# A hybrid decoder layer on one core: another order of the front, two-byte lookups, projection weights in column halves

## The chip, the core and the metric

The kernel runs on one core of one Trainium2 chip. A core has five engines with queues of their own: TensorE (PE in the profile, its weight loads PEld), VectorE (DVE), ScalarE (ACT), GpSimd (POOL) and SyncE (SP), which here only issues DMAs. The engines meet through semaphores; each works off its own instructions in the order in which the program put them. The metric is the device time of one execution in microseconds, as the median of repeated runs; beside it one execution was profiled.

## The reference, cut to what matters

One layer of a decoder over 512 tokens of width 1024, with 16 learned meta tokens in front. It has two residual sub-layers. The mixing sub-layer is an RMS norm, one input projection whose columns feed two groups, and one output projection:

```python
u = rmsnorm(h, norm_mix_w)
z, xbc, dt_raw, conf_in = split(u @ w_in)
y_ssd = ssd_mixer(z, xbc, dt_raw, ...)       # 16 heads in 4 groups, chunks of 128 tokens
y_conf = conformer_conv(conf_in, ...)        # a * sigmoid(g), causal conv of width 31,
                                             # LayerNorm over 1024 channels, swish
h = h + concat([y_ssd, y_conf]) @ w_out
h = h + peer_ffn(rmsnorm(h, norm_ffn_w), ...)
```

The SSD group convolves x, B and C with a width of 4, scans over chunks, multiplies by silu(z) and normalizes within each of its 4 groups. The channel sub-layer is a product-key lookup: for each token and each of 8 heads, the 16 best of 128 keys on either of two sides, then the 16 best of the 256 sums of these, give 16 of 16384 experts:

```python
v1, i1 = top_k(s1, 16); v2, i2 = top_k(s2, 16)
cand = v1[..., :, None] + v2[..., None, :]
top_s, pos = top_k(cand, 16)                 # expert = 128 * i1[row] + i2[column]
gate = softmax(top_s)
y = sum over experts of gelu(x . w_down[e]) * gate * w_up[e]
```

A final RMS norm ends the layer.

## The kernel before

Every large product is done in three matmuls of a reduced fp32 form: both operands are split in a high part and a remainder, and mm3 (lines 159 to 162) multiplies high by high, high by rest and rest by high into one PSUM bank. Weights are split by wsplit (line 176): SP loads the raw block, ACT copies it to the high part (line 181) and writes its negative to the low part (182), and a DMA that POOL issues adds the raw block again from DRAM to the low part (183). There are two raw and two split buffers, taken in turn.

The order of work inside each engine is not written by hand. The program calls its operations in an order, gives some of them a higher or lower priority (early and late), and a planner with a cost model arranges each engine's queue; DMAs stand in the queue of the engine that issues them. The stages are:

1. Start (lines 187 to 282). Five token tiles (four of 128 and the meta tokens, in the order MO) are loaded, normalized and transposed to uT. The z weights of group 0 and the dt columns are loaded apart and split by z_split (203).
2. Projection blocks in the order of the list ORDER (44): z0 to z3 (z_block, 312: tokens as rows, 256 columns of one group, then silu), x0 to x7 (x_block, 349: channels as rows; 0 to 3 are x, 4 and 5 are B, 6 and 7 are C, with the convolution of width 4 on DVE, lines 361 and 362) and c0 to c7 (c_block, 397: 128 gate and 128 value channels, then GLU at 406 and 407, then 30 taps on DVE, line 413, and sums for the LayerNorm, all marked late). The matmuls of x and c blocks come from proj_ct (285). An SSD group (ssd, 501) is called as soon as its x and z blocks and x4 to x7 are there; its operations are marked early. A group's result goes to DRAM, yD (548).
3. Output (590 to 670). y_split (587 on) transposes and splits y; out_part(b) (608) multiplies a quarter of the mixed channels by a quarter of w_out and adds it into h1 at 620. Parts 0 and 1 take SSD groups 0 and 1, then 2 and 3, read back from yD. Parts 2 and 3 take the conformer channels after the LayerNorm (638 to 663). Then comes the second norm with transposes (581) and splits (264).
4. Queries (775 to 792): product with the keys and the first top 16 by top16 (742: two passes of MAX8 at 743 and 746, FIND_INDEX8 at 744 and 747, MATCH_REPLACE8 at 745).
5. second(t) (825), for each token tile: the sums of a staircase of 50 candidates per head (pairs, 813) in two tables, scores and expert numbers; the top 16 of the scores; then the expert numbers of the 16 places by a one-hot compare with 0 to 49 (836), a product with the table of numbers (838) and a sum (839), in two halves of 3200 elements.
6. Gate maps (916): for tokens of tiles 0 to 2 a dense 128 x 128 map of gates per token is built from two-byte one-hots (924 to 927) by small matmuls (932, 933). Tile 3 goes another way: single experts are gathered by POOL (873) and applied on DVE (889, 896), some between gate maps.
7. All experts (986 on) for tiles 0 to 2: down projection (753) and up projection (963). 88 of the 128 down blocks are done ahead, with high priority, from stage 5 on.

The layout matters in one place: the split output operands (hl, 574) share memory with uT, so that no output part can be prepared before the last projection has read uT.

Of the kernel before, what the change touches and what calls it, by code (L numbers as in the profile page):

```python
# [43 lines left out]
ORDER = "z0 x4 x5 x6 x7 x0 c0 c1 x1 c2 x2 c3 z1 x3 c4 c5 z2 c6 z3 c7".split()  # L44
# [21 lines left out]
def pack(inputs):  # L66
# [9 lines left out]
    for k in range(8):  # L76
        blocks.append(np.concatenate([w_in[:, ca + 128 * k:ca + 128 * k + 128],
                                      w_in[:, cg + 128 * k:cg + 128 * k + 128]], 1))
    wb = np.stack(blocks)
    win = ac(wb.reshape(19, 8, 128, 256).transpose(0, 2, 1, 3))  # L80
# [37 lines left out]
def body(ctx, tc, I, out):  # L118
# [57 lines left out]
    def wsplit(raw, src, n=2048):  # L176
# [4 lines left out]
        S.activation(wh, raw, AF.Copy)  # L181
        S.activation(wl, wh.bitcast(F32), AF.Copy, scale=-1.0)
        G.dma_start(wl, src, accum_op=OP.add)
        return wh, wl
# [5 lines left out]
    load(xt[0], I["x"][0:128])  # L190
    cst = con(C_N)
    load(cst, I["cst"])
    load(wmix, bcast(I["nw"][0], 1024))
    zraw = mem(F0, 2176)
    zsrc = I["wzdt"].rearrange("p c n -> p (c n)")
    load(zraw[:, :1088], zsrc[:, :1088])
    load(xm[:NM], I["meta"])
    load(zraw[:, 1088:], zsrc[:, 1088:])
# [17 lines left out]
    def next_w():  # L216
        while worder and len(raws) < 2:
            src = I["win"][worder.pop(0)].rearrange("p c n -> p (c n)")
            raws.append((wload(src), src))
        raw, src = raws.pop(0)  # L220
        return wsplit(raw, src)
# [43 lines left out]

    for n, t in enumerate(MO):
# [7 lines left out]
        for half in range(2):  # L274
# [7 lines left out]
            split_to(uTh[:, half * 4:half * 4 + 4, c0:c0 + parts], uTl[:, half * 4:half * 4 + 4, c0:c0 + parts], pv)  # L282


    def proj_ct(wh, wl, j):
        p0, p1 = ps("pa"), ps("pa")
        for dc in range(8):
            sh = wh[:, dc * 256 + j * 128:dc * 256 + j * 128 + 128]
            sl = wl[:, dc * 256 + j * 128:dc * 256 + j * 128 + 128]
# [5 lines left out]
    A0 = S0 + 5120  # L295
    XS = [mem(o, 1280).rearrange("p (c n) -> p c n", c=5) for o in (A0, S0)]
    ZB = [mem(o, 1024).rearrange("p (t n) -> p t n", t=4) for o in (A0 + 1280, S0 + 1280)]
# [9 lines left out]
    yD = dram.tile([4, 128, 1024], F32, name="yD")  # L307


    dtraw = con(80)  # L310

    def z_block(k):
        if k == 0:
            zn = 272
            wh, wl = zsplit
        else:
            zn = 256
            wh, wl = next_w()
        for t in MO if k == 0 else range(4):
            p = ps("pa")  # L320
            c0 = NM + 128 * t if t >= 0 else 0
            z0 = 0 if t >= 0 else 256
            for dc in range(8):
                mm3(p[:, z0:zn], uTh[:, dc, c0:c0 + 128], uTl[:, dc, c0:c0 + 128],
                    wh[:, dc * zn + z0:dc * zn + zn], wl[:, dc * zn + z0:dc * zn + zn], dc == 0, dc == 7)
            if k == 0:
                V.tensor_copy(dtraw[:, 16 * (t + 1):16 * (t + 2)], p[:, 256:272])
            if t < 0:
                continue
            zt = ZB[k % 2][:, t, :]  # L330
            S.activation(zt, p[:, :256], AF.Tanh, scale=0.5)
            V.scalar_tensor_tensor(zt, zt, 1.0, p[:, :256], op0=OP.add, op1=OP.mult)
# [64 lines left out]
    def c_block(k):  # L397
        wh, wl = next_w()
        g0, g1 = proj_ct(wh, wl, 1)
        S.activation(sig[:, 0:272], g0[:, :272], AF.Tanh, scale=0.5)  # L400
        S.activation(sig[:, 272:528], g1[:, :256], AF.Tanh, scale=0.5)
        a0, a1 = proj_ct(wh, wl, 0)
# [99 lines left out]
    def ssd(g):  # L502
# [4 lines left out]
        for c in range(5):  # L507
# [11 lines left out]
            if c > 0:  # L519
# [18 lines left out]
                y_ = ybs[n % 3]  # L538
# [9 lines left out]
                load(yD[c - 1, :, 256 * g:256 * g + 256], y_)  # L548
# [36 lines left out]
    yh = [mem(B0 + 512 * k, 512) for k in range(4)]  # L585
# [22 lines left out]
    def out_part(b):  # L608
        for hf in range(2):
            po = [ps("pa") for _ in range(4)]  # L610
            src = I["wout"][hf, b].rearrange("p k n -> p (k n)")
            wh, wl = wsplit(wload(src), src)
            for t in range(4):
                for k in range(4):
                    sh, sl = hl((b % 2) * 4 + k)
                    mm3(po[t], sh[:, 128 * t:128 * t + 128], sl[:, 128 * t:128 * t + 128],
                        wh[:, 512 * k:512 * k + 512], wl[:, 512 * k:512 * k + 512], k == 0, k == 3)
            for t in range(4):
                hh = h1[t][:, 512 * hf:512 * hf + 512]
                V.tensor_tensor(hh, hh, po[t], op=OP.add)  # L620

    with early(YP):
        n = 0
        for g in range(2):
            for t in range(4):
                load(yq[n % 4], yD[t, :, 256 * g:256 * g + 256])
                y_split(yq[n % 4], t, g, 1)
                n += 1
        for t in range(4):
            load(h1[t], I["x"][128 * t:128 * t + 128])  # L630
        out_part(0)
        for t in range(4):
            load(yh[t], yD[t, :, 512:1024])
            y_split(yh[t], t, 2, 2)
        out_part(1)


    with early(LNP):
        p = ps()
        for c0, (a_, b_) in ((0, (sumd, convo[:, 7, :])), (4, (sumq, sq7[0]))):  # L640
            for t in range(4):
                ts = slice(128 * t, 128 * t + 128)
                E.matmul(p[:, c0 + t:c0 + t + 1], a_[:, ts], ones[:, 0:1], start=True, stop=False)
                E.matmul(p[:, c0 + t:c0 + t + 1], b_[:, ts], ones[:, 0:1], start=False, stop=True)
        mom = stat(8)
        V.tensor_scalar(mom, p[:, 0:8], 1.0 / D, None, op0=OP.mult)
        dl = mom[:, 0:4]
# [19 lines left out]
    out_part(2)  # L667
    out_part(3)
# [41 lines left out]
    idxf = v5(rmem(1024))  # L710
    cS = rmem(400).rearrange("p (h k) -> p h k", h=8)
    cI = rmem(400).rearrange("p (h k) -> p h k", h=8)
    h16 = lambda a: a.rearrange("p (h k) -> p h k", h=8)
    ts_, posu, posf, gate, ef, ei, i1f, i2f = [rmem(128) for _ in range(8)]
# [5 lines left out]
    oneh = mem(P0, 3200).rearrange("p (h k c) -> p h k c", h=4, k=16)  # L720
# [92 lines left out]
    def pairs(eng, o, A, B, op=OP.add):  # L813
        off = 0
        for a in range(5):
            nb = 16 // (a + 1)
            eng.tensor_tensor(o[:, :, off:off + nb], A[:, :, a:a + 1].to_broadcast([128, 8, nb]), B[:, :, 0:nb], op=op)
            off += nb
        eng.tensor_tensor(o[:, :, off:off + 6].rearrange("p h (a b) -> p h a b", a=3),
                          A[:, :, 5:8, None].to_broadcast([128, 8, 3, 2]),  # L820
                          B[:, :, None, 0:2].to_broadcast([128, 8, 3, 2]), op=op)
        off += 6
        eng.tensor_tensor(o[:, :, off:off + 8], A[:, :, 8:16], B[:, :, 0:1].to_broadcast([128, 8, 8]), op=op)

    def second(t):
        V.tensor_copy(idxf[:, t], idxu[:, t])
        V.tensor_scalar(idxf[:, t, 0], idxf[:, t, 0], 128.0, None, op0=OP.mult)
        pairs(V, cS, vals[:, t, 0], vals[:, t, 1])
        pairs(V, cI, idxf[:, t, 0], idxf[:, t, 1])
        for h in range(8):  # L830
            top16(cS[:, h, :], ts_[:, 16 * h:16 * h + 16], posu.bitcast(U32)[:, 16 * h:16 * h + 16],
                  mrb[h % 4][:, 0:50])
        V.tensor_copy(posf, posu.bitcast(U32))
        for hf in range(2):
            hs = slice(4 * hf, 4 * hf + 4)
# [204 lines left out]
```

## Time and profile before

| what | value |
|---|---|
| median of 3 runs | 1749.32 us (1747.53 to 1750.86) |
| the profiled execution | 1744.54 us, its span 1742.8 us |
| granted TensorE clock, mean | 0.969 |
| PE busy | 1642.9 us, 94% of the span |
| DVE busy | 1446.8 us, 83% |
| ACT busy | 767.2 us, 44% |
| POOL busy | 394.3 us, 23% |

A row of a group gives line, engine, operation, output and input, shapes and count, then the busy time and the mean of one in nanoseconds, then idle time before it. A row of the timeline gives start and duration in microseconds, then the instruction, and in brackets the idle time before it and what ended it. Instructions of one engine overlap a little at their ends, so that durations are slightly longer than the distance of two starts. A busy PE is not a PE at its peak: the count of its matmuls in a stretch says how fast it went.

### The profile page before, as it was taken

How to read it: one execution, taken by the hardware profiler on the slowest of the kernel's cores; microseconds unless marked ns; L12 is line 12 of the kernel's file. 1: busy time of each engine (PE TensorE's matmuls, PEld its weight loads, DVE VectorE, ACT ScalarE, POOL GpSimd, SP SyncE). 2: the span in 40 equal slices, each digit the busy share in tenths (PEclk: the TensorE clock that was granted, in tenths of full speed). 3: DMA queues.
4: the chain of work that ended last, by engine and by line, in shares of the span. 5: the costliest groups of instructions: out<-in, count | busy, mean ns of one | idle time of the engine just before them, and what ended most of it. 6: DMA issues, size and time to landing. Idle time of an engine off the chain costs nothing.

```text
span 1742.8 us, 26076 instructions
## 1 busy us (share of the span) xinstructions
PE 1642.9 (94%) x9529; PEld 1485.8 (85%) x9529; DVE 1446.8 (83%) x2873; ACT 767.2 (44%) x1117; POOL 394.3 (23%) x317
## 2 busy tenths in 40 slices
PE   6999999758989999989999999999999999999997
PEld 6999899637778899979988988888888899999996
DVE  4559999995359999999888988888888888888885
ACT  5655555434333334424655873333333333333333
POOL 1001011110000002423333003223222255444540
PEclk9999999867999999989999999999999999999999
DMA  6766567443532346768897789999999999999992
GB/s 207 170 156 155 130 153 186 135 117 82 145 106 73 97 159 232 265 211 284 296 310 288 271 290 375 342 347 364 343 341 366 325 322 364 345 351 342 327 333 81
DMA packets 163025, 426.43 MB, mean 245 GB/s; under 512 B 14144, under 2 KB 80960, under 8 KB 154832
## 3 DMA queue, kind: packets, MB, share of 16 engines
q1 hardware_dynamic: 122144, 262.22, 42.9%
q0 software_dynamic: 40752, 162.55, 30.2%
q8 instruction: 74, 1.21, 0.3%
q14 instruction: 55, 0.45, 0.1%
HBM read 382.24 MB, written 42.47 MB: 244 GB/s over the span
## 4 chain that ended last, share of the span: by engine, by line
PE 74%; DMA 10%; DVE 6%; issue 5%; ACT 3%; POOL 2%; SPq 0%; POOLq 0%; DVEq 0%; ACTq 0%
PE pa L162 16%; PE pa L161 16%; PE pa L160 16%; PE pb L162 6%; PE pb L160 6%; PE pb L161 6%; DMA MR<-win 3%; DVE M L413 3%; DMA M<-wu,M 3%; POOL M L873 1%; DMA MR<-wout 1%; PE pb L932 1%; PE pb L933 1%; DMA M<-wd,M 1%; PE pb L786 1%
## 5 line engine op out<-in xcount | busy, mean ns | idle before, releaser
L161 PE MATMUL pa<-MR 128*128 128x512 f32 (+3 forms) x2120 | 729.0, 344 | 5.1 <-DMA MR<-wout 5.1
L160 PE MATMUL pa<-MR 128*128 128x512 f32 (+3 forms) x2120 | 728.8, 345 | 5.3 <-ACT M L761 2.5
L162 PE MATMUL pa<-MR 128*128 128x512 f32 (+3 forms) x2120 | 690.2, 345 | 10.0 <-DVE MR L739 6.1
L162 PEld LDWEIGHTS pa<-MR 128*128 128x128 f32 x2120 | 402.4, 190 | 43.1 <-DVE MR L739 6.6
L160 PEld LDWEIGHTS pa<-MR 128*128 128x128 f32 x2120 | 404.1, 191 | 37.4 <-ACT M L761 3.4
L161 PEld LDWEIGHTS pa<-MR 128*128 128x128 f32 x2120 | 403.5, 190 | 36.3 <-DMA MR<-wout 6.3
L738 ACT ACTIVATE MR<-M 128x1024 fp32r<-128x1024 f32 (+1 forms) x264 | 286.0, 1084 | 289.9 <-PE pa L161 122.0
L739 DVE TENSOR_TENSOR MR<-M,MR 128x1024 fp32r<-128x1024 f32 (+1 forms) x264 | 329.3, 1250 | 45.2 <-ACT MR L738 44.3
L873 POOL DMA_INDIRECT M<-wd,M x128 | 171.4, 1339 | 491.5 <-DVE M L889 229.3
L873 POOL DMA_INDIRECT M<-wu,M x128 | 173.6, 1356 | 363.7 <-DVE M L896 215.5
L160 PE MATMUL pb<-MR 128*128 128x384 f32 (+1 forms) x576 | 206.9, 359 | 0.0
L161 PE MATMUL pb<-MR 128*128 128x384 f32 (+1 forms) x576 | 206.6, 359 | 0.0
L162 PE MATMUL pb<-MR 128*128 128x384 f32 (+1 forms) x576 | 205.5, 359 | 0.0
L959 ACT ACTIVATE MR<-M 128x384 fp32r<-128x384 f32 x128 | 66.9, 523 | 264.8 <-issue 208.4
L896 DVE SCALAR_TENSOR_TENSOR M<-M 128x1024 f32<-128x1024 f32 x128 | 163.6, 1278 | 17.9 <-DMA M<-wu,M 17.6
L413 DVE SCALAR_TENSOR_TENSOR M<-M 128x512 f32<-128x512 f32 x240 | 170.6, 740 | 2.4 <-ACT M L411 2.2
L889 DVE SCALAR_TENSOR_TENSOR M<-M 128x1024 f32<-128x1024 f32 x128 | 154.4, 1216 | 6.4 <-DMA M<-wd,M 6.3
L960 DVE TENSOR_TENSOR MR<-M,MR 128x384 fp32r<-128x384 f32 x128 | 71.0, 556 | 59.1 <-ACT MR L959 59.1
L161 PEld LDWEIGHTS pb<-MR 128*128 128x128 f32 x576 | 108.1, 188 | 11.4
L160 PEld LDWEIGHTS pb<-MR 128*128 128x128 f32 x576 | 108.1, 188 | 11.3
L935 ACT ACTIVATE M<-pb 128x512 f32<-128x512 f32 x96 | 97.0, 1159 | 46.2 <-PE pb L933 43.5
L162 PEld LDWEIGHTS pb<-MR 128*128 128x128 f32 x576 | 108.1, 188 | 10.4
(217 smaller groups left out, 1521.4 us busy)
## 6 DMA issues: line engine op xcount, KB each, us to landing
M<-wdT SPq DMA_DIRECT2D x128, 512.0 KB, 5.1
M<-wu SPq DMA_DIRECT2D x128, 512.0 KB, 6.7
GD<-M SPq DMA_DIRECT2D x40, 512.0 KB, 6.2
M<-GD SPq DMA_DIRECT2D x32, 640.0 KB, 7.9
M<-win SPq DMA_DIRECT2D x19, 1024.0 KB, 4.8
MR<-win POOLq DMA_DIRECT2D x19, 1024.0 KB, 8.2
HD<-M SPq DMA_DIRECT2D x88, 192.0 KB, 4.0
M<-HD SPq DMA_DIRECT2D x88, 192.0 KB, 6.2
```

The lines of the kernel that those rows point to most:

```text
L160: E.matmul(o, lh, rh, start=first, stop=False)
L161: E.matmul(o, lh, rl, start=False, stop=False)
L162: E.matmul(o, ll, rh, start=False, stop=last)
L413: V.scalar_tensor_tensor(o, gl[:, j:j + 512], cw[:, j:j + 1], o, op0=OP.mult, op1=OP.add)
L738: S.activation(wh, raw, AF.Copy)
L739: leng.tensor_tensor(wl, raw, wh.bitcast(F32), op=OP.subtract)
L873: r = G.indirect_dma_start(out=g, out_offset=None, in_=src, in_offset=bass.IndirectOffsetOnAxis(ap=e3[:, k:k + 1], axis=0))
L889: use(V.scalar_tensor_tensor(g, g, 1.0, x2s, op0=OP.mult, op1=OP.mult, accum_out=dots[:, k:k + 1]))
L896: use(V.scalar_tensor_tensor(h1[3], g, act3[:, k:k + 1], h1[3], op0=OP.mult, op1=OP.add))
L935: S.activation(gb.rearrange("p i t -> p t i")[:, c:c + 4, :], p.rearrange("p (t i) -> p t i", t=4), AF.Copy, scale=1.0 / GS)
L959: S.activation(sh, sf, AF.Copy)
L960: V.tensor_tensor(sl, sf, sh.bitcast(F32), op=OP.subtract)
```

## The change

- ORDER becomes z0 c0 x4 c1 x5 x6 c2 x7 x0 z1 x1 c3 c4 z2 x2 c5 z3 x3 c6 c7.
- z0 is no block of its own: each token tile's share is computed right after the tile's transposes; z_split is called one tile earlier; the norm row is loaded ahead of the constants, and the second half of the z weights ahead of the meta tokens.
- The weight blocks lie in memory as two halves of 128 columns, and wsplit works on each half by itself (two copies and one accumulating DMA each). In a conformer block the gate columns are the first half.
- SSD group 3 stays in SBUF (YL); groups 0 to 2 still go through yD and are read back one group at a time.
- out_part takes a list: parts 2 and 3 are accumulated in one PSUM group, with the second half of the columns ordered by token tile.
- The LayerNorm sums of blocks 0 to 6 and of block 7 are separate matmuls into separate columns.
- In second(t) the candidates are laid out as ten rows of eight (80 instead of 50 per head), the table of expert numbers is gone, and the two key indices are looked up from row and column in two-byte numbers.

```diff
-ORDER = "z0 x4 x5 x6 x7 x0 c0 c1 x1 c2 x2 c3 z1 x3 c4 c5 z2 c6 z3 c7".split()
+ORDER = "z0 c0 x4 c1 x5 x6 c2 x7 x0 z1 x1 c3 c4 z2 x2 c5 z3 x3 c6 c7".split()
...
+        m = n // parts
+        for j in range(parts):
+            js = slice(m * j, m * j + m)
+            S.activation(wh[:, js], raw[:, js], AF.Copy)
+            S.activation(wl[:, js], wh[:, js].bitcast(F32), AF.Copy, scale=-1.0)
+            G.dma_start(wl[:, js], src[:, js], accum_op=OP.add)
...
-        if n == 1:
+        if n == 0:
             z_split()
...
+        z_tile(0, t, 272, *zsplit)
...
-                y_ = ybs[n % 3]
+                y_ = ybs[n % 3] if g < 3 else YL[c - 1]
...
-                load(yD[c - 1, :, 256 * g:256 * g + 256], y_)
+                if g < 3:
+                    load(yD[c - 1, :, 256 * g:256 * g + 256], y_)
...
+            todo = [(t, n) for n in range(len(bs)) for t in range(4)]
+            for t, n in todo if hf == 0 else sorted(todo):
+                wh, wl = ws[n]
...
-        for c0, (a_, b_) in ((0, (sumd, convo[:, 7, :])), (4, (sumq, sq7[0]))):
+        for c0, src in ((0, sumd), (4, sumq), (8, convo[:, 7, :]), (12, sq7[0])):
...
+    def lookup(o, at, values):
+        half = lambda a: a.rearrange("p n (j s) -> p n j s", s=2)
+        io = iota16[:, 0:16].rearrange("p (j s) -> p j s", s=2)[:, None].to_broadcast([128, 128, 8, 2])
+        V.tensor_tensor(half(oneh), io, at[:, :, None, :].to_broadcast([128, 128, 8, 2]), op=OP.is_equal)
+        h4 = lambda a: a.rearrange("p (h k) c -> p h k c", h=8)
+        V.tensor_tensor(h4(picked), h4(oneh), values[:, :, None, :].to_broadcast([128, 8, 16, 16]), op=OP.mult)
+        src = picked
+        for f in fold:
+            n = f.shape[2]
+            V.tensor_tensor(f, src[:, :, 0:n], src[:, :, n:2 * n], op=OP.add)
+            src = f
+        V.tensor_tensor(o[:, :, None], src[:, :, 0:1], src[:, :, 1:2], op=OP.add)
...
-        V.tensor_copy(posf, posu.bitcast(U32))
-        for hf in range(2):
-            hs = slice(4 * hf, 4 * hf + 4)
-            V.tensor_tensor(oneh, iota50[:, None, None, :].to_broadcast([128, 4, 16, 50]),
-                            h16(posf)[:, hs, :, None].to_broadcast([128, 4, 16, 50]), op=OP.is_equal)
-            V.tensor_tensor(oneh, oneh, cI[:, hs, None, :].to_broadcast([128, 4, 16, 50]), op=OP.mult)
-            V.tensor_reduce(h16(ef)[:, hs, :], oneh, axis=AX.X, op=OP.add)
...
+        lookup(i1f, ab[0], idx16[:, 0])
+        lookup(i2f, ab[1], idx16[:, 1])
```

More of the change, by code (lines that the diff above doesn't have):

```diff
@@ L174, in body, with wsplit @@
     hk_ = [0]
-    def wsplit(raw, src, n=2048):
+    def wsplit(raw, src, n=2048, parts=1):
         k = hk_[0] % 2
@@ L190, in body @@
     load(xt[0], I["x"][0:128])
+    load(wmix, bcast(I["nw"][0], 1024))
     cst = con(C_N)
     load(cst, I["cst"])
-    load(wmix, bcast(I["nw"][0], 1024))
     zraw = mem(F0, 2176)
@@ L306, in body @@
     xws = [mem(W0 + 5376 + 256 * k, 256) for k in range(3)]
-    yD = dram.tile([4, 128, 1024], F32, name="yD")
-    dtraw = con(80)
+    YL = [mem(o, 256) for o in (S0 + 4608, S0 + 4864, F0 + 3728, F0 + 3984)]
+    yD = dram.tile([4, 128, 768], F32, name="yD")
     def z_block(k):
         if k == 0:
[L314 to L332, printed above, removed]
+            return
+        zn = 256
+        wh, wl = next_w()
+        for t in range(4):
+            z_tile(k, t, zn, wh, wl)
     Bt = mem(B0, 2048).rearrange("p (c n) -> p c n", c=4)
@@ L606, in body, with out_part @@
     x2s = mem(XS0, 1024)
-    def out_part(b):
+    def out_part(bs):
         for hf in range(2):
             po = [ps("pa") for _ in range(4)]
-            src = I["wout"][hf, b].rearrange("p k n -> p (k n)")
-            wh, wl = wsplit(wload(src), src)
-            for t in range(4):
[L614 to L628, printed above, removed]
+            ws = []
+            for b in bs:
+                src = I["wout"][hf, b].rearrange("p k n -> p (k n)")
+                ws.append(wsplit(wload(src), src))
+            todo = [(t, n) for n in range(len(bs)) for t in range(4)]
+            for t, n in todo if hf == 0 else sorted(todo):
+                wh, wl = ws[n]
+                for k in range(4):
+                    sh, sl = hl((bs[n] % 2) * 4 + k)
+                    mm3(po[t], sh[:, 128 * t:128 * t + 128], sl[:, 128 * t:128 * t + 128],
+                        wh[:, 512 * k:512 * k + 512], wl[:, 512 * k:512 * k + 512],
+                        n == 0 and k == 0, n == len(bs) - 1 and k == 3)
+                if n == len(bs) - 1:
+                    hh = h1[t][:, 512 * hf:512 * hf + 512]
+                    V.tensor_tensor(hh, hh, po[t], op=OP.add)
@@ L629, in body, with y_group @@
+    with early(YP):
+        def y_group(g):
+            for t in range(4):
+                load(yq[t], yD[t, :, 256 * g:256 * g + 256])
+                y_split(yq[t], t, g, 1)
+        y_group(0)
+        y_group(1)
         for t in range(4):
             load(h1[t], I["x"][128 * t:128 * t + 128])
-        out_part(0)
+        out_part([0])
+        y_group(2)
         for t in range(4):
-            load(yh[t], yD[t, :, 512:1024])
-            y_split(yh[t], t, 2, 2)
-        out_part(1)
+            y_split(YL[t], t, 3, 1)
+        out_part([1])
@@ L810, in body @@
     assert GRES - R0 >= 5120 and GRES + 7168 <= REND
[L813 to L823, printed above, removed]
```

101 lines of the change are left out of this document (63 added, 38 removed).

## The prediction

> **What bounds the kernel now.** I read first the span and the granted-clock row of the page, then the whole span cut into stages.
>
> ```profile
> span 1742.8 us, 26076 instructions
> PEclk9999999867999999989999999999999999999999
> ```
> The profiled execution took 1744.5 us, 1.7 more than its span. Its clock is down in two places, slices 8 to 10 (305 to 436 us) and slice 20. The stages (a row: stretch, its length, busy time of PE, PEld, DVE, ACT and POOL with their counts, granted clock, DMA share, GB/s):
>
> ```profile
> 0.00:41.00 41.00, 26.30 (x182) 25.29 (x183) 18.64 (x54) 20.82 (x35) 4.48 (x10) 1.00 0.64 206
> 41.00:120.00 79.00, 76.40 (x627) 75.53 (x626) 41.59 (x84) 50.63 (x82) 5.32 (x7) 1.00 0.68 164
> 120.00:300.00 180.00, 173.92 (x1391) 168.95 (x1390) 171.03 (x318) 96.75 (x172) 20.02 (x22) 0.98 0.61 155
> 300.00:397.00 97.00, 61.58 (x302) 48.51 (x300) 93.79 (x191) 37.66 (x87) 10.08 (x10) 0.73 0.49 129
> 397.00:500.00 103.00, 93.06 (x415) 77.88 (x416) 48.58 (x85) 43.63 (x59) 6.73 (x9) 0.90 0.43 114
> ...
> 606.00:740.00 134.00, 133.00 (x771) 132.64 (x770) 133.93 (x383) 55.11 (x76) 29.72 (x14) 1.00 0.64 215
> 740.00:780.00 40.00, 32.38 (x168) 31.24 (x167) 38.29 (x101) 10.19 (x15) 7.63 (x6) 0.87 0.60 200
> 780.00:880.00 100.00, 99.00 (x662) 96.42 (x661) 90.36 (x115) 53.85 (x72) 37.16 (x20) 1.00 0.86 293
> 880.00:940.00 60.00, 52.12 (x363) 48.21 (x362) 47.10 (x61) 30.52 (x37) 20.88 (x9) 0.91 0.86 299
> 940.00:1042.00 102.00, 100.44 (x882) 93.75 (x881) 93.24 (x137) 82.47 (x96) 8.93 (x5) 1.00 0.80 281
> 1042.00:1742.80 700.80, 689.61 (x3257) 598.15 (x3255) 581.42 (x872) 250.03 (x349) 243.30 (x206) 0.99 0.92 329
> ```
> PE sets the end nearly everywhere. It has three holes. At 0 to 41 it waits for its first operands. At 300 to 500 it is busy 154.6 of 200 us, partly at half clock, while DVE is full (93.79 of 97) until 397. At 740 to 940 DVE is nearly full and PE drops matmuls. DVE has its own hole early: 41.59 of 79 us at 41 to 120. The convolution's taps, line 413, 30 to a block, show why:
>
> ```profile
> 41.00:120.00 79.00, 0.00 (x0) 1.00 0.68 164
> 120.00:300.00 180.00, 111.96 (x158) 0.98 0.61 155
> 300.00:397.00 97.00, 58.63 (x82) 0.73 0.49 129
> ```
> All 240 of them, 170.6 us of DVE, lie behind 120, because the first conformer block is seventh in the order. The end of this stage, DVE first:
>
> ```profile
> 307.25 0.40 DVE L515 TENSOR_TENSOR M<-M 16x256 f32<-16x256 f32 x1
> ...
> 308.91 0.42 DVE L406 SCALAR_TENSOR_TENSOR M<-M,pa 128x272 f32<-128x272 f32 x1
> ...
> 390.21 0.42 DVE L544 SCALAR_TENSOR_TENSOR M<-M 128x256 f32<-128x256 f32 x1
> ...
> 393.76 2.31 DVE L413 SCALAR_TENSOR_TENSOR M<-M 128x512 f32<-128x512 f32 x3
> ```
> ```profile
> 408.93 0.17 DVE L646 TENSOR_SCALAR M<-pb 128x8 f32<-128x8 f32 x1 [4.68 <-PE pb L644]
> ...
> 429.89 1.28 DVE L663 TENSOR_TENSOR MR<-M,MR 128x512 fp32r<-128x512 f32 x2
> ...
> 482.51 0.69 DVE L620 TENSOR_TENSOR M<-M,pa 128x512 f32<-128x512 f32 x1 [0.46 <-PE pa L162]
> ...
> 496.38 1.29 DVE L264 TENSOR_TENSOR MR<-pb,MR 128x512 fp32r<-128x512 f32 x2 [3.32 <-ACT MR L263]
> ```
> The last projection is consumed at 309, the last SSD group runs from 307 to 390, the last tap ends at 396. Then come the LayerNorm sums (409), the first normalized block (430), the last output-projection add (482.5) and the last split of the second norm (497.7). PE's waits, whole span (total, times, longest):
>
> ```profile
> PE pa L591 <- DMA M<-yD: 21.5, 6, 6.9
> ...
> PE pa L161 <- DMA MR<-wout: 5.1, 3, 2.6
> ```
>
> **The change, front.** *Start.* z0 now runs tile by tile between the transposes, the weight split is asked for one tile earlier, the norm row loads ahead of the constants. z0's first matmul and the reading of its last tile before:
>
> ```profile
> 21.47 0.57 PE L160 MATMUL pa<-MR 128*128 128x272 f32 x1
> ```
> ```profile
> 40.45 0.36 ACT L331 ACTIVATE M<-pa 128x256 f32<-128x256 f32 x1
> ```
> PE idles 41 - 26.3 = 14.7 us in this stage, nearly all ahead of 21.5; I put the new first matmul at 15. At the second stage's pace (79 us for 627, 0.126 us each) z0's 96 wide and 24 narrow matmuls take 15 us, so it ends near 30 instead of 40, 10 us that count only if DVE uses them. The eight operations of the weight split wait for its load; behind them on ACT and DVE stand the first tile's square and scaling if the planner puts them there, and then the 10 are lost.
>
> *Conformer blocks.* c0 is moved past x4 to x0, and with it its weight load in SP's queue, two ACT copies, an accumulating load in POOL's queue, 96 matmuls (12.1 us) and the taps on DVE. c0's taps can start at 30 + 12 = 42 instead of 120. From there DVE is never short of work: c0 alone has 30 taps (170.6 / 8 = 21 us), c1 follows two blocks later, and the x blocks come between. DVE's work up to 397 is 18.64 + 41.59 + 171.03 + 93.79 = 325 us; about 21 of it lies ahead of 42. The other 304 at the efficiency of the stage in which DVE was already loaded (171.03 of 180, 95%) take 320 us: the last tap ends near 362 instead of 396. What is late next is c7's own projection (309 before, about 300 now), and its 21 us of taps behind that end at 321, so DVE's load decides.
>
> *After the taps.* Before: 13 us to the sums, 21 to the first normalized block, 52.6 to the last add, 15.2 to the last split, 101.6 in all. In the 34 us ahead of 430 PE was working off the output part of groups 2 and 3, which had waited for the DRAM round trip of yD (part of the 21.5 us above). Group 3 now stays in SBUF (4 stores of 16 and the 256-column loads fall away; 12 small loads remain), and its last block x3 is projected two blocks ahead of the end rather than z3 one block ahead. So I expect that part to be done at about 365, beside the last taps. The sums of the first seven blocks are done ahead; eight of the 16 matmuls remain, and PE is not in their way: 4 us. To the first block: 17, since DVE's eight pairs of line 658 and 659 remain. Output parts 2 and 3: same 192 matmuls, same four weight splits, eight adds fewer; 52.6 less the 5.1 waited for weights is 48. Strictly by tile, the second half would need the fourth split after 12 matmuls (0.25 us each, 3 us) instead of 48, with a refill of 12 us still running: up to 9 us in which everything behind on PE waits; none if the planner puts part 2 of all tiles first, which I take. The tail: with the second half ordered by tile only the last tile's norm is exposed, 10 instead of 15.2. Sum 4 + 17 + 48 + 10 = 79. The front ends at 362 + 79 = 441 instead of 497.7: **57 us**.
>
> Bounds: PE's work in 300 to 500 at full clock is 61.58 x 0.73 + 93.06 x 0.90 = 129 us of 200, so 71 plus the 10 at the start, 81, cannot be passed. If only the start and the tail gain it is 15.
>
> *Weight halves.* 19 accumulating loads become 38, ACT's two copies become four (DMA issues: KB each, us to landing).
>
> ```profile
> M<-win SPq DMA_DIRECT2D x19, 1024.0 KB, 4.8
> MR<-win POOLq DMA_DIRECT2D x19, 1024.0 KB, 8.2
> ```
> ```profile
> L181 ACT ACTIVATE MR<-M 128x2048 fp32r<-128x2048 f32 x27 | 51.7, 1915 | 61.4 <-PE pa L162 46.4 <-PE pa L161 15.0
> ```
> Refilling a buffer takes 1.9 + 1.9 + 8.2 = 12 us beside a block of 12.1 us, two buffers. A half costs between 4.1 (in proportion) and 8.2 (as the whole). Two of them, if served one behind the other, take 8.2 to 16.4 per block; below 12.1 they stay hidden. I take 5.5, hidden, worth nothing (the half that is needed first comes earlier, but PE did not wait). The Trainium skill, "DMA: Bandwidth & Descriptors", section "Anatomy of one DMA — SWDGE (gpsimd) path", speaks against halves: a fixed 2.0 us per transfer besides its bytes at 436 GB/s. That makes 4.4 for the whole, where the row above has 8.2, so the trace does not bear the figure out; its ratio of two halves to one whole (6.4 to 4.4), put on 8.2, would make 11.9, by my estimate still hidden.
>
> **The change, lookups.** In each of four token tiles the one-hot compare, product and sum over 50 candidates in fp32 give way to two 16-wide lookups in two-byte numbers.
>
> ```profile
> L838 DVE TENSOR_TENSOR M<-M 128x3200 f32<-128x3200 f32 x8 | 27.8, 3478 | 0.0
> L836 DVE TENSOR_TENSOR M<-M 128x3200 f32<-128x3200 f32 x8 | 27.8, 3475 | 0.0
> L839 DVE TENSOR_REDUCE M<-M 128x64 f32<-128x3200 f32 x8 | 27.8, 3473 | 0.0
> ```
> ```profile
> L927 DVE TENSOR_TENSOR M<-M 128x1024 f16<-128x1024 f16 x96 | 62.0, 684 | 0.6
> ...
> L744 DVE FIND_INDEX8 M<-M 128x8 uint32<-128x128 f32 x64 | 17.9, 284 | 0.0
> ...
> L744 DVE FIND_INDEX8 M<-M 128x8 uint32<-128x50 f32 x32 | 6.1, 198 | 0.0
> ```
> Removed per tile: 6 x 3.475 = 20.9, and the second candidate table with its casts, 13 operations, at line 744's 198 ns 2.6. The first table takes three operations instead of seven, one of them longer, 0.4 saved. Added: a lookup is compare and product over 2048 (by line 927, 1.37 each), folds over 1024, 512, 256 and 128 (0.68 + 0.37 + 0.25 + 0.21), 4.25, twice 8.5; ten operations on the positions, at 0.2 and a little, 2.2; top-16 over 80 instead of 50, 40 operations longer by (284 - 198) / 78 x 30 = 33 ns, 1.3. The net is 23.9 - 12.0 = 12 us, 48 us of DVE in all; if the lookups ran at the fp32 pace of line 836 (1.09 ns an element) they would take 13.7 and it would be 27.
>
> What that is worth is read from PE, which this DVE work feeds. Wide matmuls in thirds (line 160 alone):
>
> ```profile
> 740.00:780.00 40.00, 19.96 (x56) 11.25 (x56) 0.87 0.60 200
> ...
> 880.00:940.00 60.00, 25.52 (x72) 14.57 (x72) 0.91 0.86 299
> 940.00:1042.00 102.00, 47.02 (x136) 25.60 (x136) 1.00 0.80 281
> ```
> 606 to 740 is PE at full rate: 771 in 134, 0.174 us. 740 to 780 lost 40 - 168 x 0.174 = 10.8. The last stretch gives the small gate-map matmuls: (102 - 408 x 0.174) / 474 = 0.065. 880 to 940 lost 60 - 216 x 0.174 - 147 x 0.065 = 12.8. So 23.6 at most, however much DVE is freed; nothing at least, if the gathers and not DVE make the holes. The first hole lies among the lookups themselves, the second among gate maps and gathers; I take the first and under half of the second, **16 us**. After 1042 nothing changes.
>
> **Sum.** 1744.5 - 57 - 16 = 1671.5 on the profiled execution. The median of the runs, 1749.3, lies 4.8 above it; on that footing 1676.
>
> **The rivals.** *The last SSD group takes the taps' place.* It needed 83 us from 307 to 390, sharing DVE. Now it can start only when x3, eighteenth of 20, is through, near 285; with DVE loaded all the time it may need 95 and end at 380, and the output part of groups 2 and 3 (8 us of transposes and 22 of matmuls) stands at 410, in front of the last parts in PE's queue. Those then end at 410 + 48 and the front at 468, a gain of 30, with 8 in the middle: 1711. For it: the group's chain alternates between PE and DVE. Against: its DVE work has priority over the taps, and z3 came later before.
>
> *All holes close.* Front 81, middle 24: 1644. Against: PE's clock row dips even after short waits.
>
> *The halves are as dear as the whole* (slower). At 8.2 each, one behind the other in POOL's queue, a block needs 16.4 for its weights against 12.1 of PE: 4.3 us more in each of 19 blocks, 82 us, and the DVE gain of the front (34) goes with it since taps arrive later: 1749.3 + 82 - 23 - 16 = 1792. It decides from 6.05 us a half; at 8 the time passes the old one even with the order's full gain (1749.3 - 73 + 19 x 3.9 = 1750). For it: 8.2 for 1 MB is far from proportional to the 4.8 of a plain load. Against: the two halves overlap unless one queue serialises them, which no row shows.
>
> *The order does nothing*, because a planner orders the instructions and the taps are marked late: then DVE would stay idle early and the gain be 16 or less, 1733 to 1749. Against: before, the first taps came behind 120, right after the seventh block, though marked late.
>
> **How the numbers follow.** Forecast 0.60, its own range 1649 to 1706 (front 35 to 76, middle 8 to 24); SSD rival 0.18; all holes 0.07; no order 0.06, half of which is no change; dear halves or another loss of that kind 0.09. A measurement of this kernel can tell about 0.2%, 3.5 us, from no change. Faster 0.60 + 0.18 + 0.07 + 0.03 = 0.88, same 0.03, slower 0.09. The range, 1643 to 1738, leaves out the dear halves, most of no order and the ends of the others.
>
> **What would show it.** Right: taps in the 41 to 120 stretch and DVE over 90% busy there, the last tap near 362, the last split of the second norm near 441, start of the steady expert loop near 970 instead of 1042, and 700 us after it as before. The lookups near 8.5 us a tile. Wrong: PE waits for the accumulating loads of win over 4 us in all, or a wait of the output transposes for SSD after the last tap, or PE holes between 600 and 1000 as large as before though DVE idles.

## The result and the profile after

The changed kernel takes 1708.1 us (median of 4 runs, 1702.1 to 1710.5) beside 1748.9 for the kernel before on the same chip: a ratio of 0.976, interval 0.973 to 0.979. It is faster by 41 us; 73 were forecast. The profiled execution took 1709.6, its span is 1707.9. It is 34.9 us shorter than the profiled execution before (1744.5), so the marks below account for 35 of the 41 us; the rest is spread between executions.

The page of the changed kernel, its span and its row of granted clock:

```profile
span 1707.9 us, 26157 instructions
PEclk9999999589999999999999999999999999999999
```

The same stretches of the whole span as in the prediction (length, busy time of PE, PEld, DVE, ACT and POOL with their counts, granted clock, DMA share, GB/s):

```profile
41.00:120.00 79.00, 79.00 (x656) 78.93 (x656) 71.42 (x128) 47.22 (x83) 11.12 (x13) 1.00 0.80 186
...
300.00:397.00 97.00, 82.41 (x356) 66.25 (x357) 82.50 (x180) 41.02 (x93) 10.45 (x11) 0.74 0.44 121
...
940.00:1042.00 102.00, 100.60 (x573) 93.18 (x572) 54.97 (x74) 43.49 (x58) 18.32 (x11) 1.00 0.73 244
```

and line 422, the taps, alone (line 413 before):

```profile
41.00:120.00 79.00, 46.10 (x64) 1.00 0.80 186
```

DVE's early hole is closed: 71.42 of 79 us instead of 41.59, 46.1 of them taps where there were none. In 940 to 1042 DVE is now half idle and PE is the limit, though the expert loop now begins within this stretch. The marks of the front, on DVE (start, length, line):

```profile
358.46 1.53 DVE L422 SCALAR_TENSOR_TENSOR M<-M 128x512 f32<-128x512 f32 x2
...
371.28 0.41 DVE L553 SCALAR_TENSOR_TENSOR M<-M 128x256 f32<-128x256 f32 x1
...
377.41 0.17 DVE L659 TENSOR_SCALAR M<-pb 128x8 f32<-128x8 f32 x1 [4.92 <-PE pb L657]
...
398.03 0.68 DVE L677 TENSOR_TENSOR MR<-M,MR 128x512 fp32r<-128x512 f32 x1
...
404.36 0.69 DVE L634 TENSOR_TENSOR M<-M,pa 128x512 f32<-128x512 f32 x1 [0.83 <-PE pa L162]
...
455.13 0.69 DVE L634 TENSOR_TENSOR M<-M,pa 128x512 f32<-128x512 f32 x1 [0.23 <-PE pa L162]
...
469.23 1.29 DVE L267 TENSOR_TENSOR MR<-pb,MR 128x512 fp32r<-128x512 f32 x2 [3.55 <-ACT MR L266]
```

The last tap ends at 360 (396 before), the last SSD operation at 371.7 (390.6), the last add of the output part of groups 2 and 3 at 405 (433.0), the last split of the second norm at 470.5 (497.7). So 36 us were won by the last tap and 27 were left at the front's end. The first operation of the steady expert loop that uses gate values (line 957 before, 979 after), in the two kernels:

```profile
1025.86 0.50 DVE L957 TENSOR_TENSOR M<-M 128x320 f32<-128x320 f32 x1 [0.50 <-DMA M<-GD]
```
```profile
991.21 0.49 DVE L979 TENSOR_TENSOR M<-M 128x320 f32<-128x320 f32 x1
```

It comes 34.7 us earlier: 27.2 from the front, 7.5 from the middle. From there to the end it is 716.9 before and 716.7 after: nothing changes there.

### The profile page after: what moved, and what is told of

Same layout as the page of the kernel before. It is cut to its first block, busy times and chain, and to the rows that moved or that the text cites. A ratio compares the mean times of both kernels' runs of the same rounds, so it can differ in the third digit from the quotient of the medians.

```text
span 1707.9 us, 26157 instructions
## 1 busy us (share of the span) xinstructions
PE 1643.6 (96%) x9529; PEld 1487.2 (87%) x9529; DVE 1397.6 (82%) x2864; ACT 770.7 (45%) x1155; POOL 397.6 (23%) x336
## 3 DMA queue, kind: packets, MB, share of 16 engines
q8 instruction: 74, 1.21, 0.3%
## 5 line engine op out<-in xcount | busy, mean ns | idle before, releaser
L162 PEld LDWEIGHTS pa<-MR 128*128 128x128 f32 x2120 | 404.0, 191 | 38.3 <-DVE MR L755 5.4
L161 PEld LDWEIGHTS pa<-MR 128*128 128x128 f32 x2120 | 404.9, 191 | 34.9 <-DMA MR<-wout 4.6
L895 POOL DMA_INDIRECT M<-wu,M x128 | 177.7, 1388 | 387.4 <-DVE M L918 255.6
L895 POOL DMA_INDIRECT M<-wd,M x128 | 156.2, 1220 | 471.8 <-DVE M L911 209.6
L918 DVE SCALAR_TENSOR_TENSOR M<-M 128x1024 f32<-128x1024 f32 x128 | 163.5, 1278 | 15.4 <-DMA M<-wu,M 15.1
L911 DVE SCALAR_TENSOR_TENSOR M<-M 128x1024 f32<-128x1024 f32 x128 | 154.6, 1218 | 14.0 <-DMA M<-wd,M 13.7
```

Of the source, the lines that this page charges most:

```text
L161: E.matmul(o, lh, rl, start=False, stop=False)
L162: E.matmul(o, ll, rh, start=False, stop=last)
L895: r = G.indirect_dma_start(out=g, out_offset=None, in_=src, in_offset=bass.IndirectOffsetOnAxis(ap=e3[:, k:k + 1], axis=0))
L911: use(V.scalar_tensor_tensor(g, g, 1.0, x2s, op0=OP.mult, op1=OP.mult, accum_out=dots[:, k:k + 1]))
L918: use(V.scalar_tensor_tensor(h1[3], g, act3[:, k:k + 1], h1[3], op0=OP.mult, op1=OP.add))
```

## The experiments

All ratios are to the kernel before, run on the same chip in the same session. Two of the kernels below (old lookups, no gathers) have the same front code as the changed kernel; its end came at 465.4 and 467.3 in their profiles, at 470.5 in the changed kernel's. Differences under about 5 us in that mark therefore say nothing. Part of this spread is there already at the last GLU, which starts between 293.5 and 296.9 in the profiles with the new order of blocks and the weights in halves, unless x3 is moved. What follows the front takes 1236.4 to 1241.0 us in the seven profiles of kernels that do the whole computation and have the changed kernel's code from there on.

### The lookups: one kernel without, one with nothing else

The changed kernel with the second lookup of before, and the kernel before with the new one: the function `second` with its helper and its buffers exchanged, no other line.

```diff
-        lookup(i1f, ab[0], idx16[:, 0])
-        lookup(i2f, ab[1], idx16[:, 1])
+            V.tensor_tensor(oneh, iota50[...], h16(posf)[...], op=OP.is_equal)
+            V.tensor_tensor(oneh, oneh, cI[...], op=OP.mult)
+            V.tensor_reduce(h16(ef)[:, hs, :], oneh, axis=AX.X, op=OP.add)
```

> The changed kernel with the old second lookup (one compare, product and sum over 50 candidates): the front alone. Theory (the lookups gave about 8 us, the front 27): the last split of the second norm stays at 470, the steady expert loop starts about 999 instead of 991, the time is about 8 above the changed kernel, 1716. If the lookups are worth what I forecast, 16: 1724. If the middle's gain came from something else in the change: 1708.

> The kernel before with the new second lookup alone. Theory: the front ends at 497.7 as before, one-hot results come about 48 us earlier in DVE time, the expert loop starts 8 us earlier than 1026, the time is about 1741. By the forecast's 16 it is 1733; if DVE's time there is covered altogether it stays at 1749.

Old lookup in the changed kernel: 1708.8 us, ratio 0.981 (0.979 to 0.983), against 0.976 (0.973 to 0.979) with the new one; what follows its front takes 1712.7 - 465.4 = 1247.3 us of its span, against 1707.9 - 470.5 = 1237.4. The profiled execution was the longest of its six (1707.3 to 1714.4). New lookup alone: 1738.2 us, ratio 0.999 (0.997 to 1.001), which is not told from no change. The sums over 606 to 1042, of the kernel before and of the new lookup alone, show why:

```profile
sum 436.00, PE 416.93 PEld 402.25 DVE 402.93 ACT 232.13 POOL 104.32; mean PE 138.98 PEld 134.08 DVE 134.31 ACT 77.38 POOL 34.77
```
```profile
sum 436.00, PE 420.38 PEld 405.33 DVE 358.00 ACT 231.63 POOL 86.72; mean PE 140.13 PEld 135.11 DVE 119.33 ACT 77.21 POOL 28.91
```

DVE has 45 us less to do (48 forecast) and PE gets 3.5 us more done. The lookups are worth about 2 us alone, which is within the noise, and 6 to 11 behind the new front (1247.3 against 1236.4 to 1241.0), on one profile; the two ratios differ by 0.005, 9 us, with intervals that touch.

### No gathers among the gate maps

```diff
-SPRATE = (4.0, 1.03, 3.33, 0)
+SPRATE = (0, 1.6, 3.33, 0)
```

> The changed kernel with no gathers of the token-by-token experts among the gate maps; the 48 that stood there go into the later loops at a quicker pace. It tells what holds the rest of PE's losses in the middle (24 us between 585 and 991, 11 of them at 805 to 885). Theory that the waits of DVE for the gathers hold them: PE's loss falls to 10 to 16 and the expert loop starts 8 to 14 us earlier than 991 (977 to 983). If it is DVE's own work and the lookups' chain alone, the loss stays at 20 to 24. What the 48 gathers then cost in the expert loop is not part of the test: the time may be 1695 to 1710 by the first, 1705 to 1715 by the second.

400 us of the middle, from the same point of the work (584 and 581), in the changed kernel and without the gathers:

```profile
585.00:985.00 400.00, 385.06 (x2675) 371.39 (x2674) 342.12 (x744) 221.62 (x277) 87.75 (x54) 0.99 0.79 271
```
```profile
581.00:981.00 400.00, 400.00 (x2795) 389.85 (x2794) 299.05 (x680) 227.11 (x287) 9.84 (x7) 1.00 0.64 220
```

PE has no idle time left, with the lookups as they are in the changed kernel. The first weight split of the loop comes at 967.2 instead of 992.4, 25 us earlier (3 of them from the front). But the loop then takes 753.8 us instead of 715.5, and the whole 1720.8 (ratio 0.986, 0.982 to 0.990), above what I expected: the 48 gathers cost 38 there. The start of the loop moved by more than the first expectation's 8 to 14. In the changed kernel DVE waits for gathers only in this stretch, 28.8 us in all (last column of the two rows of its page), and works 59.7 us on them there:

```profile
L918 DVE SCALAR_TENSOR_TENSOR M<-M 128x1024 f32<-128x1024 f32 x128 | 163.5, 1278 | 15.4 <-DMA M<-wu,M 15.1
...
L911 DVE SCALAR_TENSOR_TENSOR M<-M 128x1024 f32<-128x1024 f32 x128 | 154.6, 1218 | 14.0 <-DMA M<-wd,M 13.7
```

So the holes in the middle belong to the gathers. Whether to DVE's work on them, its waits for them or their share of the DMA traffic, this run does not tell: it takes all three away. The place is still right for them.

### The old order, and x3 earlier

The changed kernel with the order of before; with x3 sixteenth and c2 after x1; and with x3 sixteenth, c2 in its place and SSD group 2 written behind x3:

```diff
-ORDER = "z0 c0 x4 c1 x5 x6 c2 x7 x0 z1 x1 c3 c4 z2 x2 c5 z3 x3 c6 c7".split()
+ORDER = "z0 x4 x5 x6 x7 x0 c0 c1 x1 c2 x2 c3 z1 x3 c4 c5 z2 c6 z3 c7".split()    (old order)
+ORDER = "z0 c0 x4 c1 x5 x6 x7 x0 z1 x1 c2 z2 x2 c3 z3 x3 c4 c5 c6 c7".split()    (x3 early)
+ORDER = "z0 c0 x4 c1 x5 x6 c2 x7 x0 z1 x1 c3 z2 x2 z3 x3 c4 c5 c6 c7".split()    (x3 ahead)
-        while left and {"x4", "x5", "x6", "x7", "x%d" % left[0], ...} <= done:
+        while left and {"x4", "x5", "x6", "x7", "x%d" % max(left[0], left[0] // 2 * 3), ...} <= done:    (x3 ahead)
```

> The changed kernel with the old order of blocks, everything else new. Theory: nearly all of the front's 27 us is the order, which lets the taps start early; without it the last tap is back near 390 and the time is 1728 to 1736. If the z0 by tile, the group kept in SBUF and the early sums carry the gain, it stays below 1715.

> The changed kernel with another order: z0 c0 x4 c1 x5 x6 x7 x0 z1 x1 c2 z2 x2 c3 z3 x3 c4 c5 c6 c7, so that the last SSD group's block x3 is sixteenth instead of eighteenth. Theory that the last SSD group and the output part of groups 2 and 3 behind it set the front's end: group 3 ends before 345 instead of 371, LayerNorm sums come within 6 us of the last tap, the last split of the second norm near 450 instead of 470, time about 1690. If the taps decide, the last tap stays at or behind 360 and the front at 465 to 470: 1704 to 1708. If DVE runs short of work early or the taps are pushed back by as much: 1708 or more.

> The changed kernel with x3 sixteenth in the order (z0 c0 x4 c1 x5 x6 c2 x7 x0 z1 x1 c3 z2 x2 z3 x3 c4 c5 c6 c7, so that c2 keeps its place) and SSD group 2 written behind x3, so that x3's transposes stand ahead of SSD group 2 in PE's queue. In the changed kernel they stand behind its last chunk, which is why group 3 began at 318 though x3 was projected near 277. Theory that PE's queue between the last projection (297) and the last tap is the place of the loss: group 3 ends before 355, output part 1 is worked off before 385, the last split of the second norm is near 450 to 458, time 1688 to 1696. If DVE's total work decides (it is full until 371 either way): last of taps and SSD stays at 365 to 372, the front at 462 to 470, time 1700 to 1708. If SSD taken later or taps pushed back cost more than this: 1710 or more, as with x3 moved up before.

Old order: 1723.8 us, ratio 0.989 (0.985 to 0.993). Its last tap ends at 386.4, 26 us later than with the new order, yet its front ends at 481.5, only 11 later:

```profile
385.62 0.74 DVE L422 SCALAR_TENSOR_TENSOR M<-M 128x512 f32<-128x512 f32 x1
...
480.18 1.29 DVE L267 TENSOR_TENSOR MR<-pb,MR 128x512 fp32r<-128x512 f32 x2 [4.11 <-ACT MR L266]
```

So the order is not nearly all of the front's gain, as I had it, and the time lies between the two expectations. The order is worth 11 to 16 us at the front's end (481.5 against 465.4 to 470.5), and it is the order's own gain, 26 us at the last tap, that is in part given back behind the taps.

x3 earlier made it worse both times: 1721.9 (0.990, 0.987 to 0.994) and 1717.3 (0.984, 0.980 to 0.987). The last SSD operation ended at 380 and 375, not before 345 and 355, the last tap at 391 both times. DVE ran short of taps in between: 23.93 of 40 us at 120 to 160 with c2 moved back, and with c4 and c5 moved back in 200 to 300, where this is the sum of the changed kernel's row and then that of x3 ahead:

```profile
sum 100.00, PE 95.65 PEld 91.73 DVE 95.33 ACT 56.79 POOL 14.39; mean PE 47.83 PEld 45.87 DVE 47.67 ACT 28.39 POOL 7.20
```
```profile
sum 100.00, PE 95.95 PEld 91.28 DVE 76.48 ACT 53.62 POOL 14.35; mean PE 47.98 PEld 45.64 DVE 38.24 ACT 26.81 POOL 7.17
```

With x3 ahead, group 3 began at 280 instead of 318 and still ended at 375. My theory that x3's place in PE's queue is the loss falls; that DVE must never be short of taps fits both runs.

### What stands behind the taps

Five kernels on the stretch from 360 to 470. Half of the last block's taps left out:

```diff
-            for j in range(1, 31):
+            for j in range(1, 31 if k < 7 else 16):
```

> The changed kernel with 15 of the 30 taps of the last convolution block left out (so that block of the result is wrong by these taps): 11 us less of DVE work behind the last GLU, with everything else in place. DVE is busy 59 of 60 us in 300 to 360. Theory that DVE's work sets the end of both the taps and the last SSD group, and everything behind follows: the last tap near 349 and the last SSD operation near 361 instead of 360 and 371, the front ends near 460, time 1697 to 1700. If the last SSD group goes by its own chain between PE, ACT and DVE: its end stays at 368 to 371, the front at 468 to 470, time 1706 to 1708. If PE's backlog of output parts 0 and 1 alone sets what follows, the group ends earlier and the front still at 466 to 470.

The taps end at 340.2, 20 us earlier, and the last SSD operation does not follow:

```profile
337.89 2.31 DVE L422 SCALAR_TENSOR_TENSOR M<-M 128x512 f32<-128x512 f32 x3
...
368.23 0.42 DVE L553 SCALAR_TENSOR_TENSOR M<-M 128x256 f32<-128x256 f32 x1
...
460.42 1.29 DVE L267 TENSOR_TENSOR MR<-pb,MR 128x512 fp32r<-128x512 f32 x2 [3.58 <-ACT MR L266]
```

The group goes by its own chain (its end is that of the second expectation), and the LayerNorm sums wait behind it: their first use came at 370.8, 30 us after the last tap. Yet the front's end, 461.7, and the time, 1700.3 (0.973, 0.970 to 0.976), are near those of the first: the sums came 6.6 us sooner than in the changed kernel, and output part 1 behind them was done at 397.2 instead of 405.1.

The sums put first:

```diff
-    with early(LNP):
+    with early(2500):
         p = ps()
         for c0, src in ((0, sumd), (4, sumq), (8, convo[:, 7, :]), (12, sq7[0])):
             ...
+    with early(LNP):
```

> The changed kernel with the LayerNorm sums given the highest priority: the same 32 small matmuls now stand after the first of the last SSD group's final matmuls, and the two row broadcasts follow before any matmul of the output part of groups 2 and 3, where 22 of that part stood ahead of them. Theory that PE's backlog of output part 1 decides (done at 404 in any case): the first normalized block comes 3 to 8 us earlier than 398, the front ends at 466 to 470, the time is 1704 to 1708. If the chain from the sums to the first normalized block decides: front 460 to 465, time 1698 to 1703.

The first normalized block came at 389.5 instead of 398.0, the last add at 453.1 instead of 455.1, the front's end at 468.4: 1710.1 us (0.980, 0.976 to 0.984). Output part 1 was done at 404.0, as in the changed kernel. A shorter chain to the first normalized block wins nothing, as the theory of PE's backlog has it.

Group 3 not waited for (its rows replaced by group 2's), and output part 1 left out:

```diff
-            y_split(YL[t], t, 3, 1)
+            y_split(yq[t], t, 3, 1)
```
```diff
-        out_part([1])
```

> The changed kernel in which the output part of groups 2 and 3 takes group 2's rows a second time in place of group 3's (so it leaves SSD group 3 out of the result): the same matmuls, the same SSD work on DVE, but nothing waits for its end. Theory that this output part, held up by SSD group 3 until 371, stands ahead of parts 2 and 3 on PE until 404: it is now done before 375, parts 2 and 3 start with the first normalized block and the front ends 6 to 14 us earlier than 470, time 1694 to 1702. If the LayerNorm chain behind the taps sets the front by itself, with parts 2 and 3 following it in any case, the front stays at 468 to 471 and the time at 1706 to 1708.

> The changed kernel without output part 1 (so it leaves the product of SSD groups 2 and 3 with their output weights out of the result; the groups themselves, their reloads, transposes and splits stay). It is 96 wide matmuls (22 us at 0.2265 each), two weight splits and eight adds less. Theory that this part, begun at 378 behind the sums and done at 404, is the backlog in front of parts 2 and 3: the row broadcasts follow the sums at once, the first normalized block comes near 391, parts 2 and 3 begin there with weights ready and end 48 later, the last split of the second norm near 452 to 456, time 1690 to 1695. If the chain of the LayerNorm or the weights of parts 2 and 3 decide, the front ends only at 463 to 470, time 1702 to 1708.

Without the wait for group 3 the front ends at 462.3 (1704.7 us, 0.978, 0.974 to 0.981): 8 us before the changed kernel's, but no more than 3 to 5 below the two other profiles of that front. The part keeps its place in PE's queue, behind the sums, and is done at 397.8, not before 375; so the run does not show what it would win if it were done early. Without output part 1 the time is 1687.2 (0.966, 0.963 to 0.969):

```profile
371.83 0.17 DVE L658 TENSOR_SCALAR M<-pb 128x8 f32<-128x8 f32 x1 [3.02 <-PE pb L656]
...
385.64 1.88 DVE L676 TENSOR_TENSOR MR<-M,MR 128x512 fp32r<-128x512 f32 x3
...
431.81 0.69 DVE L634 TENSOR_TENSOR M<-M,pa 128x512 f32<-128x512 f32 x1 [0.23 <-PE pa L162]
...
446.84 1.29 DVE L267 TENSOR_TENSOR MR<-pb,MR 128x512 fp32r<-128x512 f32 x2 [4.48 <-ACT MR L266]
```

Its last tap ended at 356.4 and its last SSD operation at 368.0, as with the part; the front ends at 448.1, 17 to 22 us earlier than in the three profiles with it. That is the price of this part where it stands: 96 matmuls (22 us at full rate) with two weight splits and eight adds, which the run does not part.

The other profiles say the same. In the kernel before, the part's last add is this:

```profile
432.30 0.68 DVE L620 TENSOR_TENSOR M<-M,pa 128x512 f32<-128x512 f32 x1
```

From the end of the part's last add to the end of the front it is 64.7 us there, 65.5 in the changed kernel, and 62.0 to 66.9 in all 13 profiles of kernels that have the part, while their last taps end anywhere from 340 to 396. The front's end follows the end of this part, not the last tap.

Parts 2 and 3 accumulated apart, as before the change:

```diff
-    out_part([2, 3])
+    out_part([2])
+    out_part([3])
```

> The changed kernel with output parts 2 and 3 accumulated apart, as before the change (eight more adds, no order by tile). My forecast took 4 to 5 us for the order by tile in the second half, in the tail between the last add and the last split of the second norm. Measured, the tail was 15.4 after and 15.2 before, so the theory now is that joining the parts gained nothing: the front ends within 3 us of 470 and the time is 1705 to 1712. If joining them gains: 1713 to 1718. If the order by tile costs a wait for the fourth weight split: 1699 to 1704.

1707.8 us (0.979, 0.975 to 0.983), the last add at 448.6 and the last split's end at 463.5: 15 us of tail, as with the parts joined. Joining them gained nothing that can be seen. No kernel that does the whole computation can be told from the changed one as faster.

### Whole weight splits

```diff
-        return wsplit(raw, src, parts=2)
+        return wsplit(raw, src)
```

> The changed kernel with the projection weights split whole again (19 accumulating loads of 1 MB, 8.2 us each in the kernel before, instead of 38 of 512 KB at 6.7). Theory: both are hidden behind the 12 us that PE works on a block, so the stages up to the last GLU keep their places within 2 us and the time stays within 4 us of the changed kernel (1708). If the halves cost something, it is faster by more; if they carry part of the gain, PE's waits for the win transfers come back (3.9 us before) and the time is 1712 or more.

1717.1 us (0.985, 0.982 to 0.988). The halves were not free of effect; with whole splits PE waits for them again (total, times, longest):

```profile
PE pa L162 <- DMA MR<-win: 7.2, 5, 2.1
...
PE pa L161 <- DMA MR<-win: 1.6, 2, 0.8
```

In the kernel before there was one such row, and in the changed kernel there is none:

```profile
PE pa L162 <- DMA MR<-win: 3.9, 6, 1.3
```

The last GLU starts at 305.4 instead of 296.9, the front ends at 476.6 and the span is 7.4 us longer. So the halves carry 6 to 11 us of the front's gain (476.6 against 465.4 to 470.5).

## Why the prediction was right in kind and wrong in size

The sign, the parts and the order of their sizes were right; 32 of the 73 us are missing by the medians, 38 by the profiles (30 in the front, 8 in the middle). The 27 us of the front, the 7.5 of the middle and the 1708 all lie just outside the forecast's own ranges (35 to 76, 8 to 24, 1649 to 1706). By its own steps:

*Start.* z0's first matmul came at 10.9 (15 forecast), but its last tile was read at 39.4, not 30. The start did not set the end: z0's later matmuls stand among the transposes of the last token tiles, PE's granted clock was 0.66, 0.83 and 0.83 in the 5-us steps from 20 to 35, and the last tile, computed by 37.5, was read behind two of c0's weight copies on ACT. Which of these weighs most no run shows. c0's taps start at 50, not 42. The gain went into the blocks behind.

*Conformer blocks.* "The last tap ends near 362": it ended at 360. DVE was at 90% in 41 to 120. This step held, nearly with its 95%: DVE was busy for 297 us of the 319 from 41 to 360, 93%.

*After the taps: the step that failed.* "So I expect that part to be done at about 365, beside the last taps." The output part of groups 2 and 3 was done at 404 (405 with its last add). The four terms, forecast and measured, with the kernel without this part beside them:

| from, to | before | forecast | after | without part 1 |
|---|---|---|---|---|
| last tap's end to the sums' first use | 12.9 | 4 | 17.4 | 15.4 |
| to the first normalized block | 21.0 | 17 | 20.6 | 13.8 |
| to the last output add | 52.6 | 48 | 57.1 | 46.2 |
| to the last split of the second norm | 15.2 | 10 | 15.4 | 16.3 |
| sum | 101.6 | 79 | 110.5 | 91.7 |

The first row is the last SSD group, which took the taps' place: it ends 11.7 us behind them, and the sums follow its last matmuls on PE, 5.7 us more to their first use. The forecast had the sums of the first seven blocks done ahead and eight matmuls left; the trace has no sum ahead, but 32 matmuls in one row (16 before), 6.93 us at half clock. The second and third rows are output part 1, begun at 378 and done at 404 in front of parts 2 and 3; without it the third row is 46, so the 48 was right for what it counted. PE's queue in the changed kernel:

```profile
312.63 1.94 PE L551 MATMUL pb<-M 128*128 128x64 f32 x8 [1.52 <-DVE M L546]
314.36 1.06 PE L352 MATMUL pb<-M 128*128 128x128 f32 x4
...
369.15 1.49 PE L551 MATMUL pb<-M 128*128 128x64 f32 x8 [1.15 <-DVE M L546]
370.44 6.93 PE L657 MATMUL pb<-M 128*128 128x1 f32 x32
377.23 1.09 PE L600 MATMUL pa<-M 128*128 128x128 f32 x4
...
385.57 1.95 PE L402 MATMUL pb<-M 128*128 128x128 f32 x16
```

Behind the last SSD chunk (line 551) come the sums, the transposes (600), then the part's matmuls, with the row broadcasts (402) only in their midst. This is the rival *the last SSD group takes the taps' place*, which stood at 0.18: it had the part at 410, the front at 468, 8 us in the middle and 1711; measured were 404, 470.5, 7.5 and 1708. That its 468 is so close is partly luck: the part was done 6 us sooner and the tail was 5 us longer than it had them. Its reason was only half right. I had put the group's late start on x3's late projection; x3's transposes (line 352) stand behind group 2's last chunk on PE, yet moving them ahead brought the group's start forward by 38 us and not its end. The round trip through DRAM did go, as forecast: PE's waits for yD fell from 21.5 us to 2.3. What paces the group inside (it needs 53 us from its start at 318, and 95 with x3 ahead; PE, DVE and ACT alternate in waits of 1 to 2 us) I did not take apart, and it stays open.

*The tail.* 10 was taken for the order by tile, 15.4 measured, and 15.0 with the parts apart: the term was nothing.

*Weight halves.* "I take 5.5, hidden, worth nothing" missed a gain of 6 us or more. A refill of 12 us beside a block of 12.1 is a tie, not a cover; that the half needed first lands early breaks it is an explanation I did not test apart. The halves' own price was above the 5.5 I took:

```profile
MR<-win POOLq DMA_DIRECT2D x38, 512.0 KB, 6.7
```

It is also above 6.05, the point from which the rival of dear halves would decide if two were served one behind the other. It did not decide: the profile lists no wait of PE for a half. In the trace nine of the 38 halves were issued 4.7 to 7.8 us before the one ahead of them had landed (two issued at 208.4 and 209.4 landed at 216.0 and 219.6), so two can be under way at once. Most others were issued at about the time the one ahead landed; the 13 that ran alone or nearly so took 5.4 to 7.4 us, 5.9 in the median.

*Lookups.* A lookup costs 1.22 + 1.21 for compare and product, 0.67, 0.41, 0.28 and 0.28 for the folds (the compare's row below), 4.07 us; 4.25 was forecast.

```profile
L832 DVE TENSOR_TENSOR M<-M 128x2048 f16<-128x2048 f16 x8 | 9.8, 1221 | 0.0
```

The 16 us they were to bring PE came out as 6 to 11 here and 2 in the old front. The failed sentence is "the first hole lies among the lookups themselves": the new lookups alone gave PE 3.5 us, and in the changed kernel the holes go when the gathers go, with the lookups untouched. A sum of DVE's time saved (45 us) is no gain while PE or a gather ends the wait.

Two slips in the working decide nothing. The second place of low clock on the page is slice 18 (741 to 784 us), not slice 20. At the fp32 pace the 6016 elements of a lookup would make 13.1 us a tile and 29 in all, not 13.7 and 27.

## What to carry to other kernels

When the last of several chains is shortened, write down what ends next and, for each in-order queue, what stands in it between that event and the end: here 36 us won on one engine met 26 us of another engine's backlog. A refill that takes as long as the work beside it (12 and 12.1 us here) is not hidden; splitting it so that the first half lands early is worth trying. And before time saved on an engine is counted, ask which wait in that stretch ends last; leaving out one suspect at a time (the taps, the part, the gathers) went far to answer that here, in one profile each.

## What the runs showed of the hardware

PE's granted clock fell to half in the SSD stretch although PE never waited long. The changed kernel, 305 to 345 in steps of 5 us (stretch, length, PE busy, clock, DMA share, GB/s):

```profile
305.00:310.00 5.00, 2.94 (x12) 0.50 0.94 196
...
335.00:340.00 5.00, 5.00 (x15) 0.61 0.00 0
340.00:345.00 5.00, 5.00 (x23) 1.00 0.01 3
```

The clock fell between 301 and 302 (1.00, 0.69 and 0.50 in the 1-us steps from 300), when PE's longest wait since 296 had been 1.3 us. Its longest up to 345 is 2.3 us (for a reload of yD); between 303 and 337, with half to nine tenths of its time busy, it stayed at half, until it had been full for some 5 us. The sums ran into the next such dip, with 0.50 from 370 to 382: 6.93 us for 32 matmuls. The Trainium skill, "TensorE: Matmul & The Clock Gate", section "Part 1: The HAM clock gate (the "warmup" mystery)", gives an idle window of about 3.4 us for the fall to half rate; here the clock fell with many waits that were all shorter.

An accumulating half of 512 KB took 6.7 us in the median and a whole of 1 MB 8.2, 1.5 us apart. If a transfer costs a fixed part and a part in proportion to its bytes, about 5.2 us of either is fixed, by an estimate from these two; from the 5.9 us of the halves that ran alone it is 3.6. The Trainium skill, "DMA: Bandwidth & Descriptors", section "Anatomy of one DMA — SWDGE (gpsimd) path", would have 3.2 and 4.4, by an estimate from its formula; the 1.2 us between its two sizes is below the 1.5 to 2.3 measured, and its fixed part of 2.0 below both 3.6 and 5.2.
